# Head norms of a hybrid decoder layer gathered into one late block, and a weight load and a weight split moved

## The chip, the cores and the metric

The kernel runs on one core of one Trainium2 chip. The metric is the device time of one execution in microseconds (us); lower is better. Each kernel is timed in several runs, and the median is given. One further execution is profiled, which gives the rows below.

Of the core's engines, TensorE (PE in the profile) multiplies matrices into PSUM, VectorE (DVE), ScalarE (ACT) and GpSimd (POOL) do the rest, and SyncE (SP) issues the DMAs. Each engine takes its instructions in order, so one that waits holds all that are queued behind it. PEclk is the granted clock of TensorE as a share of the full one: 1.00 is 2.4 GHz, 0.50 is 1.2 GHz.

## The reference, cut to what matters

A decoder layer for 512 tokens of width 1024: a recurrent mixer (RG-LRU) and a sparse attention (NSA) in parallel, gates, then an MLP. All the projections come from one product with `w_in`. The part at hand is the root-mean-square norm over heads of 64 columns for the queries `q`, the selection keys `k_s` and the window keys `k_w`:

```python
def rmsnorm(x, g):
    xf = x.astype(jnp.float32)
    y = xf * lax.rsqrt(jnp.mean(xf * xf, axis=-1, keepdims=True) + NORM_EPS)
    return y.astype(x.dtype) * g

def nsa_mixer(q, k_c, v_c, k_s, v_s, k_w, v_w, ...):
    qh = rmsnorm(q.reshape(B, T, N_HEADS, hd), q_norm) * (hd ** -0.5)
    kc = rmsnorm(compress_blocks(kv(k_c), phi_k_pe, phi_k_w1, phi_k_w2), kc_norm)
    vc = compress_blocks(kv(v_c), phi_v_pe, phi_v_w1, phi_v_w2)
    ks = rmsnorm(kv(k_s), ks_norm)...
    kw = jnp.pad(rmsnorm(kv(k_w), kw_norm)...)

def hybrid_layer(x, ...):
    (u_rnn, u_gate, q, k_c, v_c, k_s, v_s, k_w, v_w, g_nsa, g_a, g_b) = jnp.split(xn @ w_in, cuts, axis=-1)
```

`compress_blocks` is a small two-layer network (weights `phi_*_w1`, `phi_*_w2`) over overlapping blocks of 32 tokens of `k_c` and `v_c`; its output is attended to as well.

## The kernel before, in words

Each product is made of three matmuls: a float32 operand is split into a rounded high part and the low rest, and high x high, high x low and low x high are summed in PSUM (`mm3`). So every weight tile, once loaded by a DMA into a raw buffer (`wraw`, two of them, filled by `raw`), is split by `split`: GpSimd or ScalarE copies out the high part (`wh`), then VectorE subtracts (`wl`). Two pairs of split buffers are in turn (WB = 2), so a split waits until TensorE has finished the tile two before.

The work runs in this order. First the 21 column tiles of the recurrent branch (`u_tiles`, in the order UO, loaded in pairs by `UW.load`), each followed by a causal convolution on VectorE (`uc`) whose rows are moved by DMAs into `ub`, and between them four blocks of the recurrence (`lru`), whose gate weights (`graw`) are loaded and split too. Then the token-major projections, by `tok_cols`: selection keys KS, selection values VS, window keys KW, window values and gates VW, and the first group of queries Q. Each uses all four PSUM banks named `lru`, one for each 128 tokens, and two or three weight pieces of at most 1024 columns. Its sink evicts the banks: `v_sink` copies the high part of the values by ScalarE and the low part by VectorE (both into `VV`); `head_norm` copies keys or queries by ScalarE (into `kn` or `qn`), squares them by ScalarE into a spare tile (`zdk` or `zdv`), and, after the last of the four banks, sums the squares by VectorE and normalizes. The norm itself is `rstd_heads`: the sum (VectorE), a scaling (VectorE), and a power of -0.5 (GpSimd, from the constant `halfs`); then VectorE multiplies each of the four blocks of 128x256.

Then come four column tiles for the compressed keys and values (class `Cols`, ZW, in the PSUM banks `mm`, with the high part copied by ScalarE), whose banks ScalarE and VectorE evict into `zdk` and `zdv`. After them comes compression itself: eight pieces of `phi_*_w1` loaded into `praw` (two buffers) and split into `pwh` and `pwl`, with matmuls of another product filled in between. Attention, the merge and the MLP follow and are as before.

The program is written in this order, but a scheduler places the instructions on each engine's queue by priorities; `tc.issue_after` holds an instruction back behind another. The queues are thus not those of the text, and the change is shown as they come out.

Of the kernel before, what the change touches and what calls it, by code (L numbers as in the profile page):

```python
# [11 lines left out]
F32 = mybir.dt.float32  # L12
F32R = mybir.dt.float32r
AF = mybir.ActivationFunctionType
# [54 lines left out]
def layer(ctx, tc, x, norm_mix, w_in, conv_w, conv_b, gate_a_w, gate_a_b, gate_x_w, gate_x_b,  # L69
# [58 lines left out]
    def split(v, a, b, pl=wp, tags=("wh", "wl"), prio=PRIO, bufs=WB, act=False):  # L128
        parts = v.shape[0]
        th = pl.tile([128, WH], F32R, name=tags[0], bufs=bufs)  # L130
        tl = pl.tile([128, WH], F32R, name=tags[1], bufs=bufs)
        h = th[:parts, :a * b].rearrange("p (a b) -> p a b", b=b)
        l = tl[:parts, :a * b].rearrange("p (a b) -> p a b", b=b)
        with tc.high_priority(offset=prio):
            if act:
                S.activation(h, v, AF.Copy)  # L136
            else:
                G.tensor_scalar(h, v, 1.0, 0.0, op0=OP.mult, op1=OP.add)  # L138
            split_last[0] = V.tensor_tensor(l, v, f32(h), op=OP.subtract).ins  # L139
        return h, l  # L140
# [101 lines left out]
    def u_half(n, hf):  # L242
        wh, wl = UW.get(n)
        run(feat_gen(p2[n], wh, wl, XH, XL, None, slice(256 * hf, 256 * hf + 256)))
# [6 lines left out]
    u_half(1, 0)  # L251
    u_half(0, 1)
    UW.load(2)
    u_half(1, 1)

    def col(src, name, parts, n):
# [256 lines left out]
    def rstd_heads(sq, nh, name, pl):  # L513
        ss = pl.tile([128, nh], F32, name=name, bufs=2)
        V.tensor_reduce(ss, sq, axis=AX, op=OP.add)
        V.tensor_scalar(ss, ss, 1.0 / 64, EPS, op0=OP.mult, op1=OP.add)
        G.tensor_tensor(ss, ss, halfs[:, :nh], op=OP.pow)
        return ss
# [39 lines left out]
        V.tensor_tensor(d4, d4, rs.unsqueeze(2).to_broadcast([128, 4, 64]), op=OP.mult)  # L558


    def head_norm(d, i, ps, pl, key):
        if i == 0:
            SQ[key] = pl.tile([128, 4, T], F32, name="zd" + "kvk"[key])[:, 0:2].rearrange("p a (b c) -> p (a b) c", c=256)
        src = ps[:, :256].rearrange("p (h d) -> p h d", d=64)
        S.activation(d[:, i], src, AF.Copy)
        S.activation(SQ[key][:, i], ps[:, :256], AF.Square)
        if i == 3:
            rs = rstd_heads(SQ.pop(key).rearrange("p i (h d) -> p (i h) d", d=64), 16, "hrs", pl)
            rv = rs.rearrange("p (i h) -> p i h", h=4)
            for n in range(4):  # L570
                V.tensor_tensor(d[:, n], d[:, n], rv[:, n].unsqueeze(2).to_broadcast([128, 4, 64]), op=OP.mult)

    def k_sink(br):
        def sink(i, ps):
# [79 lines left out]
    with pool("ph") as ph:  # L654
# [23 lines left out]
        for h in range(BC):  # L678
            bias_copies(h)
        tok_cols(COL_Q, 256, q_sink)  # L680
        w1p = {parts[0]: split(w1s.pop(parts[0]), 4, 256, ph, ("pwh", "pwl"), prio=0)}
        for n, nm in enumerate("kv"):
            z = ph.tile([128, 4, T], F32, name="zd" + nm)
            G.memset(z[64:128, :, 496:512], 0.0)
            for m in range(2):
                ps = psr.tile([128, T], F32, name="mm", bufs=3)
                wh, wl = ZW.get(2 * n + m)
                ZW.prep(2 * n + m + 1)
                run(feat_gen(ps, wh, wl, XH, XL, None))
                for gl in range(2):  # L690
                    g = 2 * m + gl
                    S.activation(z[0:64, g, :], ps[64 * gl:64 * gl + 64, :], AF.Copy)
                    V.tensor_copy(z[64:128, g, 0:496], ps[64 * gl:64 * gl + 64, 16:512])
            zd[nm] = z
        for nm, v in zip("kv", w2r):
            wh, wl = w2s[nm]
            S.activation(wh, v, AF.Copy)
            V.tensor_tensor(wl, v, f32(wh), op=OP.subtract)
# [591 lines left out]
```

## Time and profile before

| | us |
|---|---|
| median of 3 runs | 1060.33 (1060.20 to 1062.89) |
| the profiled execution | 1059.58 |
| its span in the trace | 1057.9 |
| TensorE busy | 1033.8 (98%) |
| VectorE busy | 647.4 (61%) |
| ScalarE busy | 388.6 (37%) |
| GpSimd busy | 310.3 (29%) |

The busy times are shares of the span. TensorE's is 98%, so the time is close to that of its matmuls, and the few stretches in which it rests or has a lower clock are to be looked for one by one. The stretch tables give each engine's busy time between two points; the rows of one engine in order of time tell what ended each wait.

### The profile page before, as it was taken

Reading aid. Unit: us, or ns where it says so; the run is one execution under the profiler, and the core shown is the slowest. Engines: PE = TensorE matmul, PEld = TensorE weight load, DVE = VectorE, ACT = ScalarE, POOL = GpSimd, SP = SyncE. Lnnn points to the kernel's source line nnn. Section 1 sums busy time; section 2 is a strip of 40 time slices with the busy share of each in tenths; the row PEclk is TensorE's granted clock in tenths of the full one; section 3 lists DMA queues with packets and bytes.
Section 4 is the critical chain, followed back from the end, with each engine's and each line's share of the span. In section 5 each row is a group of like instructions: output and inputs, shape, how many; then the busy total and the mean of one; then the engine's idle time right before and its main releaser. Section 6 shows DMA issues by size and latency. Waiting matters only on the chain.

```text
span 1057.9 us, 14717 instructions
## 1 busy us (share of the span) xinstructions
PE 1033.8 (98%) x5405; PEld 882.6 (83%) x5405; DVE 647.4 (61%) x1208; ACT 388.6 (37%) x808; POOL 310.3 (29%) x349
## 2 busy tenths in 40 slices
PE   6999999989999999999999999999999999999998
PEld 5777877989888898989988888888888888888886
DVE  5588989854764878868777669554333343444443
ACT  4356666413432666747657631132111111111010
POOL 4110111432231474546635423202111121111110
PEclk9999999989999999999999999999999999999999
DMA  7636333643263724334342278602323323323222
GB/s 181 147 94 197 87 108 117 140 126 126 66 189 100 229 78 122 118 114 119 69 132 91 91 243 301 210 1 80 111 89 91 109 83 116 120 80 103 97 80 80
DMA packets 110039, 127.89 MB, mean 121 GB/s; under 512 B 23087, under 2 KB 87375, under 8 KB 109967
## 3 DMA queue, kind: packets, MB, share of 16 engines
q1 hardware_dynamic: 109967, 126.94, 39.9%
q8 instruction: 43, 0.70, 0.3%
q14 instruction: 29, 0.24, 0.1%
HBM read 109.45 MB, written 15.64 MB: 118 GB/s over the span
## 4 chain that ended last, share of the span: by engine, by line
PE 90%; DVE 3%; DMA 2%; ACT 2%; issue 2%; POOL 1%; SPq 0%; DVEq 0%; ACTq 0%; POOLq 0%
PE mf L143 6%; PE mf L144 6%; PE mf L145 6%; PE am L145 5%; PE am L144 5%; PE am L143 5%; PE mi L145 5%; PE mi L143 5%; PE mi L144 5%; PE sc L922 4%; PE po L960 4%; PE pt L941 3%; PE mm L144 3%; PE mm L145 3%; PE mm L143 3%; PE lru L143 3%
## 5 line engine op out<-in xcount | busy, mean ns | idle before, releaser
L139 DVE TENSOR_TENSOR wl<-wraw,wh 128x1024 fp32r<-128x1024 f32 (+2 forms) x110 | 131.9, 1201 | 72.4 <-POOL wh L138 44.7
L138 POOL TENSOR_SCALAR wh<-wraw 128x1024 fp32r<-128x1024 f32 (+3 forms) x83 | 85.7, 1033 | 250.4 <-PE mi L144 119.1
L933 POOL TENSOR_SCALAR pp<-pp,sm,gates 128x512 f32<-128x512 f32 (+3 forms) x128 | 93.4, 737 | 68.0 <-DVE sm L931 45.2
L145 PE MATMUL am<-mwh,zl 128*128 128x512 f32 x256 | 99.3, 389 | 0.0
L144 PE MATMUL am<-mwl,zh 128*128 128x512 f32 x256 | 99.3, 389 | 0.0
L143 PE MATMUL am<-mwh,zh 128*128 128x512 f32 x256 | 98.8, 389 | 0.0
L145 PE MATMUL mi<-XH,wl 128*128 128x512 f32 x240 | 93.5, 390 | 0.3 <-DVE wl L139 0.3
L143 PE MATMUL mi<-XH,wh 128*128 128x512 f32 x240 | 93.5, 389 | 0.1
L144 PE MATMUL mi<-XL,wh 128*128 128x512 f32 x240 | 93.4, 389 | 0.0
L1233 DVE TENSOR_TENSOR zl<-Z,zh 128x512 fp32r<-128x512 f32 x32 | 36.2, 1134 | 88.4 <-ACT zh L1232 88.4
L143 PE MATMUL mm<-XH,wh 128*128 128x512 f32 (+1 forms) x216 | 81.9, 381 | 1.8 <-ACT wh L136 1.8
L144 PE MATMUL mm<-XL,wh 128*128 128x512 f32 (+1 forms) x216 | 81.7, 379 | 1.0 <-DVE XL L226 1.0
L930 ACT ACTIVATE pp<-pp,mx 128x512 f32<-128x512 f32 (+3 forms) x128 | 71.5, 561 | 29.3 <-DVE mx L928 27.2
L145 PE MATMUL mm<-XH,wl 128*128 128x512 f32 (+1 forms) x216 | 81.4, 378 | 0.5 <-DVE wl L139 0.5
L1206 DVE SCALAR_TENSOR_TENSOR Z<-mi,zr 128x512 f32<-128x512 f32 x30 | 20.7, 691 | 97.1 <-ACT zr L1205 97.1
L138 POOL TENSOR_SCALAR mwh<-wraw 128x1024 fp32r<-128x1024 f32 x32 | 34.0, 1062 | 138.4 <-PE am L145 131.3
L1232 ACT ACTIVATE zh<-Z 128x512 fp32r<-128x512 f32 x32 | 20.2, 632 | 136.5 <-PE am L144 134.4
L1205 ACT ACTIVATE zr<-mi 128x512 f32<-128x512 f32 x30 | 18.0, 600 | 141.7 <-PE mi L145 136.9
L928 DVE CUSTOM_DVE_ANT_0 pp<-sc,BT 128x512 f32<-128x512 f32 (+3 forms) x128 | 59.0, 484 | 15.3 <-PE pt L941 7.4
L947 ACT ACTIVATE PH<-pt 128x512 fp32r<-128x512 f32 (+1 forms) x96 | 49.3, 524 | 33.6 <-PE pt L941 33.1
L948 DVE TENSOR_TENSOR PL<-pt,PH 128x512 fp32r<-128x512 f32 (+1 forms) x96 | 55.9, 592 | 6.6 <-ACT PH L947 6.4
L922 PE MATMUL sc<-KK,QS 128*128 128x512 f32 (+3 forms) x256 | 57.8, 334 | 0.0
(299 smaller groups left out, 2687.1 us busy)
## 6 DMA issues: line engine op xcount, KB each, us to landing
wraw<-in_w_in_dram SPq DMA_DIRECT2D x26, 1024.0 KB, 5.2
wraw<-in_w_mlp_in_dram SPq DMA_DIRECT2D x16, 1024.0 KB, 5.6
wraw<-in_w_mlp_out_dram SPq DMA_DIRECT2D x16, 1024.0 KB, 4.8
tab_p<-tab_t SPq DMA_DIRECT2D x16, 320.0 KB, 5.0
wraw<-in_proj_a_dram SPq DMA_DIRECT2D x8, 640.0 KB, 5.3
BT<-tab_p SPq DMA_DIRECT2D x16, 256.0 KB, 2.8
wraw<-in_proj_b_dram SPq DMA_DIRECT2D x4, 1024.0 KB, 6.4
wraw<-in_w_out_dram SPq DMA_DIRECT2D x4, 1024.0 KB, 5.3
```

Of the source, the lines that this page charges most:

```text
L138: G.tensor_scalar(h, v, 1.0, 0.0, op0=OP.mult, op1=OP.add)
L139: split_last[0] = V.tensor_tensor(l, v, f32(h), op=OP.subtract).ins
L143: PE.matmul(ps, lh, rh, start=start, stop=False)
L144: PE.matmul(ps, lh, rl, start=False, stop=False)
L145: return PE.matmul(ps, ll, rh, start=False, stop=stop)
L922: ins = PE.matmul(ps[:, cs], grp.Q[r][:, ts], grp.K[br][:, hl, :128 * (i + 1)], start=hl == 0, stop=hl == 1)
L928: V.tensor_tensor_reduce(out=pp[:, cs], in0=ps[:, cs], in1=BTS[h][:, 384 - 128 * i:], scale=1.0, scalar=3e38, op0=OP.add, op1=OP.min, accu ...
L930: S.activation(pp[:, cs], pp[:, cs], AF.Exp, bias=mx, scale=-1.0, accum_out=sm)
L933: G.tensor_scalar(pp[:, cs], pp[:, cs], sm, gt, op0=OP.mult, op1=OP.mult)
L947: S.activation(ph, pv, AF.Copy)
L948: V.tensor_tensor(pl, pv, f32(ph), op=OP.subtract)
L960: PE.matmul(po[:, 128 * kt:], VV[:, kt, br, g], P[n][:, KT0[kt]:KT0[kt] + 128 * (4 - kt)], start=False, stop=br == 1 and kt == 3 and n == 1)
```

## The change

`head_norm` keeps the copy, the squares and the sum of squares, which it now writes into 16 of the 48 columns of one tile. A new function `head_norms` does the rest for KS, KW and Q together, and stands in the text behind the four column tiles of compression: scaling, a root by ScalarE (`AF.Sqrt`, which needs another activation table), a reciprocal, and one Newton step of four VectorE instructions, then the twelve multiplies. The power on GpSimd goes away for these three. The split of compression's first weight piece is to be issued behind the last split before it, that of the queries' second half. In the recurrent branch, the third pair of column weights is loaded earlier.

```diff
     u_half(0, 1)
     UW.load(2)
+    UW.load(4)
     u_half(1, 1)
...
+    SS, SD = [], []
+
     def head_norm(d, i, ps, pl, key):
...
         if i == 3:
-            rs = rstd_heads(SQ.pop(key).rearrange("p i (h d) -> p (i h) d", d=64), 16, "hrs", pl)
-            rv = rs.rearrange("p (i h) -> p i h", h=4)
+            if not SS:
+                SS.append(pl.tile([128, 48], F32, name="ss48"))
+            V.tensor_reduce(SS[0][:, 16 * key:16 * key + 16], SQ.pop(key).rearrange("p i (h d) -> p (i h) d", d=64),
+                            axis=AX, op=OP.add)
+            SD.append(d)
+
+    def head_norms(pl):
+
+        x, (r, t) = SS[0], (pl.tile([128, 48], F32, name=nm) for nm in ("rs48", "rt48"))
+        V.tensor_scalar(x, x, 1.0 / 64, EPS, op0=OP.mult, op1=OP.add)
+        S.activation(r, x, AF.Sqrt)
+        V.reciprocal(r, r)
+        V.tensor_tensor(t, r, r, op=OP.mult)
+        V.tensor_tensor(t, t, x, op=OP.mult)
+        V.tensor_scalar(t, t, -0.5, 1.5, op0=OP.mult, op1=OP.add)
+        V.tensor_tensor(r, r, t, op=OP.mult)
+        rv = r.rearrange("p (b i h) -> p b i h", b=3, h=4)
+        for b, d in enumerate(SD):
             for n in range(4):
-                V.tensor_tensor(d[:, n], d[:, n], rv[:, n].unsqueeze(2).to_broadcast([128, 4, 64]), op=OP.mult)
+                V.tensor_tensor(d[:, n], d[:, n], rv[:, b, n].unsqueeze(2).to_broadcast([128, 4, 64]), op=OP.mult)
...
         tok_cols(COL_Q, 256, q_sink)
-        w1p = {parts[0]: split(w1s.pop(parts[0]), 4, 256, ph, ("pwh", "pwl"), prio=0)}
+        with tc.issue_after(split_last[0]):
+            w1p = {parts[0]: split(w1s.pop(parts[0]), 4, 256, ph, ("pwh", "pwl"), prio=0)}
...
             zd[nm] = z
+        head_norms(ph)
```

VectorE's queue from the last weight split of VS (the first row) to the second of KW, before:

```order
L139 TENSOR_TENSOR wl<-wraw,wh 128x1024
L515 TENSOR_REDUCE hrs<-zdk 128x16
L516 TENSOR_SCALAR hrs<-hrs 128x16
L571 TENSOR_TENSOR kn<-kn,hrs 128x4x64 x4
L139 TENSOR_TENSOR wl<-wraw,wh 128x1024
L582 TENSOR_TENSOR VV<-lru,VV 128x4x64
L139 TENSOR_TENSOR pwl<-praw,pwh 128x1024
L582 TENSOR_TENSOR VV<-lru,VV 128x4x64
...
L139 TENSOR_TENSOR pwl<-praw,pwh 128x1024
L582 TENSOR_TENSOR VV<-lru,VV 128x4x64 x2
L139 TENSOR_TENSOR wl<-wraw,wh 128x1024
```

And now:

```order
L139 TENSOR_TENSOR wl<-wraw,wh 128x1024
L573 TENSOR_REDUCE ss_1798<-zdk 128x16
L139 TENSOR_TENSOR wl<-wraw,wh 128x1024
L601 TENSOR_TENSOR VV<-lru,VV 128x4x64 x2
...
L601 TENSOR_TENSOR VV<-lru,VV 128x4x64 x2
L139 TENSOR_TENSOR wl<-wraw,wh 128x1024
```

The scaling, the four multiplies and both splits of compression weights have left the stretch; left out are two short splits (`w2lk`, `w2lv`) that stand in both. GpSimd's queue loses the power there and is else the same.

VectorE's queue from the splits for the first two column tiles of compression (the first row) on, before:

```order
L139 TENSOR_TENSOR wl<-wraw,wh 128x1024 x2
L515 TENSOR_REDUCE hrs<-zdk 128x16
L516 TENSOR_SCALAR hrs<-hrs 128x16
L139 TENSOR_TENSOR wl<-wraw,wh 128x1024
L693 COPY zdk<-mm 64x496
L571 TENSOR_TENSOR qn<-qn,hrs 128x256 x4
L693 COPY zdk<-mm 64x496
L139 TENSOR_TENSOR wl<-wraw,wh 128x1024
```

And now, from the scaling on:

```order
L580 TENSOR_SCALAR ss_1798<-ss_1798 128x48
L582 RECIPROCAL rs_2452<-rs_2452 128x48
...
L586 TENSOR_TENSOR rs_2452<-rs_2452,rt_2453 128x48
L590 TENSOR_TENSOR kn<-kn,rs_2452 128x4x64 x6
L139 TENSOR_TENSOR wl<-wraw,wh 128x1024
L590 TENSOR_TENSOR kn<-kn,rs_2452 128x4x64 x2
L590 TENSOR_TENSOR qn<-qn,rs_2452 128x256 x3
L713 COPY zdk<-mm 64x496
L590 TENSOR_TENSOR qn<-qn,rs_2452 128x256
L139 TENSOR_TENSOR wl<-wraw,wh 128x1024
```

The new block with its twelve multiplies stands ahead of and between the splits for the third and the fourth column tile. ScalarE's queue has the table load and the root just ahead of its copy (`wh`) for the third column tile, and a table load between the square and the tanh of compression's first activation.

SP's queue of DMAs among the constants and the gate weights, before:

```order
L276 DMA kcg<-in_kc_norm_dram 64x1 x2
...
L287 DMA pev<-in_phi_v_pe_dram 64x16x1 x2
L121 DMA graw<-in_gate_a_w_dram 112x3x336
L121 DMA graw<-in_gate_x_w_dram 112x3x336
L121 DMA wraw<-in_w_in_dram 128x8x256 x2
L341 DMA ub<-uc 112x512
```

And now:

```order
L277 DMA kcg<-in_kc_norm_dram 64x1
L121 DMA wraw<-in_w_in_dram 128x8x256
L277 DMA kcg<-in_kc_norm_dram 64x1
...
L121 DMA graw<-in_gate_a_w_dram 112x3x336
L121 DMA graw<-in_gate_x_w_dram 112x3x336
L121 DMA wraw<-in_w_in_dram 128x8x256
L342 DMA ub<-uc 112x512
```

One of the two loads of 1 MB behind the gate weights now stands between the two loads of `kcg`.

## Rows read from the trace of the kernel before

**Rows 1.** Stretch table: stretch, length, busy PE, PEld, DVE, ACT, POOL, clock, DMA.

```profile
41.40:44.90 3.50, 1.24 (x4) 0.77 (x5) 1.79 (x2) 2.67 (x3) 0.00 (x0) 1.00 1.10 333
44.90:206.90 162.00, 161.93 (x770) 131.09 (x769) 139.53 (x203) 96.21 (x135) 27.25 (x29) 1.00 0.41 118
...
213.40:218.35 4.95, 0.14 (x2) 0.03 (x1) 4.95 (x6) 0.38 (x1) 3.07 (x3) 0.92 0.02 3
218.35:224.45 6.10, 6.10 (x28) 6.10 (x29) 4.66 (x8) 0.00 (x0) 0.00 (x0) 0.50 0.62 140
224.45:300.00 75.55, 75.55 (x470) 68.81 (x469) 43.32 (x67) 26.46 (x58) 20.83 (x19) 1.00 0.42 124
```

**Rows 2.** TensorE in order of time: start, duration, instruction, idle before and releaser.

```profile
207.64 0.39 PE L144 MATMUL lru<-wl,XH 128*128 128x256 f32 x1 [0.58 <-DVE wl L139]
...
213.14 0.28 PE L144 MATMUL lru<-wl,XH 128*128 128x256 f32 x1
213.26 0.28 PE L145 MATMUL lru<-wh,XL 128*128 128x256 f32 x1
218.35 0.55 PE L143 MATMUL lru<-wh,XH 128*128 128x256 f32 x1 [4.82 <-DVE VV L582]
...
268.63 0.39 PE L143 MATMUL mm<-XH,wh 128*128 128x512 f32 x1
...
274.07 0.39 PE L143 MATMUL mm<-XH,wh 128*128 128x512 f32 x1
```

**Rows 3.** VectorE in order of time, at the start of KW.

```profile
211.96 4.78 DVE L571 TENSOR_TENSOR kn<-kn,hrs 128x256 f32<-128x256 f32 x4 [3.03 <-POOL hrs L517]
216.66 1.21 DVE L139 TENSOR_TENSOR wl<-wraw,wh 128x1024 fp32r<-128x1024 f32 x1
```

**Rows 4.** GpSimd in order of time, in the same stretch.

```profile
209.01 2.92 POOL L517 TENSOR_TENSOR hrs<-hrs,halfs 128x16 f32<-128x16 f32 x1 [2.20 <-DVE hrs L516]
...
212.91 2.39 POOL L138 TENSOR_SCALAR pwh<-praw 128x1024 fp32r<-128x1024 f32 x2
```

**Rows 5.** Early stretch, each in time: SP, POOL, ACT, DVE; page's and 0:62's loads.

```profile
24.96 1.77 SPq L276 DMA_DIRECT2D kcg<-in_kc_norm_dram  x2
...
33.71 1.05 SPq L121 DMA_DIRECT2D wraw<-in_w_in_dram  x2
...
39.10 1.03 POOL L138 TENSOR_SCALAR gwh<-graw 112x1008 fp32r<-112x1008 f32 x1 [0.62 <-DMA graw<-in_gate_x_w_dram]
46.38 0.62 POOL L368 TENSOR_SCALAR uh<-ub 112x512 fp32r<-112x512 f32 x1 [6.24 <-DMA ub<-uc]
...
42.02 1.06 ACT L136 ACTIVATE wh<-wraw 128x1024 fp32r<-128x1024 f32 x1 [9.94 <-DMA wraw<-in_w_in_dram]
...
48.84 0.74 DVE L335 SCALAR_TENSOR_TENSOR uc<-mm,cw,uc 128x509 f32<-128x509 f32 x1
...
wraw<-in_w_in_dram SPq DMA_DIRECT2D x26, 1024.0 KB, 5.2
...
wraw<-in_w_in_dram SPq DMA_DIRECT2D x4, 1024.0 KB, 7.2
```

**Rows 6.** VectorE in order of time, behind the queries.

```profile
261.40 0.17 DVE L516 TENSOR_SCALAR hrs<-hrs 128x16 f32<-128x16 f32 x1
...
265.51 0.67 DVE L693 COPY zdk<-mm 64x496 f32<-64x496 f32 x1
266.21 1.43 DVE L571 TENSOR_TENSOR qn<-qn,hrs 128x256 f32<-128x256 f32 x4
```

**Rows 7.** ScalarE in order of time: a table load, and compression's first activation.

```profile
156.12 1.28 ACT L391 ACT_TABLE_LOAD   x1
157.41 1.49 ACT L391 ACTIVATE rr<-rr 112x1536 f32<-112x1536 f32 x1
...
297.88 0.36 ACT L323 ACTIVATE hs<-lru 128x256 f32<-128x256 f32 x1
300.06 0.42 ACT L325 ACTIVATE hs<-hs 128x256 f32<-128x256 f32 x1 [1.82 <-DVE hs L324]
```

## The prediction, made from the trace of the kernel before

> **What bounds the kernel now.** I read the stretch table first, since shares of the whole span hide where TensorE rests. From 44.9 to 206.9 us TensorE is busy for 161.93 of 162.00 us, and from 224.45 to 300 for all of it [rows 1]. So what the matmuls need is the bound, and the change can win only where TensorE waits or runs slowly. Two such places lie where the diff works. In the stretch 41.4 to 44.9 TensorE is busy for 1.24 of 3.50 us. From 213.4 to 218.35 it is busy for 0.14 of 4.95, and from 218.35 to 224.45 it is busy throughout, but at a granted clock of 0.50: 28 matmuls in 6.10 us [rows 1]. Next I read TensorE's own rows at these places, for the releaser. The matmuls for the window keys (columns KW) start at 218.35, after 4.82 us, released by VectorE's eviction of VV; the last matmul before them is at 213.26 [rows 2]. Then VectorE and GpSimd in the same stretch: GpSimd takes 2.92 us from 209.01 for one power of 128x16, and VectorE, which waits 3.03 us for it, then needs 4.78 us for the four multiplies of kn [rows 3, 4]. Only behind them come KW's weight split, at 216.66, and the evictions of VV [rows 3]. TensorE needs both, as one of the four PSUM banks must be free and its weights must be there. So a short norm, in the middle of an in-order queue, holds TensorE.
>
> **The pause before KW.** The change leaves only the sum of squares there and puts power, wait and multiplies behind the first queries. From VectorE's queue go the small scaling, 3.03 us of waiting and 4.78 of multiplies, nearly 8 us [rows 3]. I follow what is late next, in the clock of the trace before. KW's first weight half needs a buffer that the first half of VS gives back just ahead of the matmul at 207.64 [rows 2]. GpSimd, no longer in a power, copies it at once, in about 1.2 us as its other copies [rows 4]; VectorE's sum of squares ends by 208.8 (211.96 - 3.03 - 0.17, the wait and the scaling [rows 3, 6]), its split of 1.21 us by 210.0, and the first VV follows. TensorE asks for them at 213.26 + 0.12 = 213.38, matmuls coming every 0.12 us there [rows 2], so 3 us are to spare. KW's second half gets its buffer at 213.4, is ready 2.4 us later (copy and split), and is wanted 48 matmuls on, at 219.1. Compression's first two copies stay where they are in GpSimd's queue (2.39 us from 212.91 before [rows 4], now about 3 us earlier) and end before that. Only their VectorE halves, 2.4 us, move behind the queries' second weight half. The loads that follow them in SP's queue move too: four loads of compression weights go behind three loads of column weights; they serve the work after the last column tile, which ends at 274.07 + 5.44 [rows 2]. The pause of 218.35 - 213.38 = 4.97 us is gone. So, if TensorE does not rest, is the slow clock: 28 matmuls at full clock are 28 x 0.12 = 3.36 us, against 6.10, so 2.74 more [rows 1]. A shorter pause earlier in this trace, 41.4 to 44.9, left the clock at 1.00 [rows 1]. **7.7 us** in sum; the lower bound is nothing (third rival), the upper is 7.7 + 0.58, the wait at 207.64 that VectorE's backlog causes [rows 2].
>
> **The early load.** The third pair of weight columns is now issued after the first kcg load, at about 25.6, and not at 33.7 [rows 5]. Before, ScalarE waited 9.94 us for it, to 42.02 [rows 5], and TensorE rested for 3.50 - 1.24 = 2.26 [rows 1]. Now ScalarE's copy is set by a buffer that TensorE frees one tile earlier (5.44 us, from 268.63 to 274.07 [rows 2]), at about 36, so that pause goes. What it costs: the load takes an issue slot (0.5 us) ahead of the small constants, and the eighth DMA after it, a pev load, waits for its landing. Eleven issues filled the time from 25.6 to 33.7, 0.74 each, so that one comes at about 31.5. By the page's median of 5.2 us the pair lands at 30.8 and holds nothing; by 7.2, the median of the kernel's start, at 32.8, and what follows is issued 1.3 us later [rows 5]. For it, one megabyte less stands between the gate weights, landed at 39.10, and the ub copies: up to 42.02, so 2.9 us. GpSimd's first use of ub, at 46.38, moves 2.9 - 0.5 = 2.4 us earlier, or 1.1 in the bad case. This matters because VectorE's uc at 48.84, queued behind it, frees the PSUM bank for the next tile but one [rows 5]. TensorE's own rest of 2.26 and VectorE's 2.4 meet: **2.3 us**, between 1.1 and 2.9; I take the upper half, since only small constants move when the load is issued.
> Whether it lasts: TensorE is full to 206.9, but VectorE is busy for 139.5 of these 162 us [rows 1], and its late split makes the wait of 0.58 at 207.64 [rows 2]. All of VectorE's work there follows from work that has moved by about the same 2.3, so I keep it.
>
> **The norms' new place.** Behind the queries VectorE now does: sum of squares (as before), scaling to 261.57 [rows 6], then, after ScalarE's root, a reciprocal and four steps on 128x48, six multiplies of kn, the split for the third column tile of compression, two more kn, three qn, a copy, one qn, the next split. No row shows a root or a reciprocal of that size. The nearest, the scaling of 128x16, took 0.17 us, and a multiply of 128x256 goes every 1.43 / 4 = 0.36 [rows 6]. Six steps are 1.0 to 2.2 us; with hand-overs I take 1.2, near the smaller, as 48 columns are nearer to 16 than to 256. The 0.36 is with GpSimd quiet; a multiply of kn under GpSimd's copies took 4.78 / 4 = 1.20 [rows 3, 4]. I take 0.36: GpSimd's power goes away, and its next copy waits for the buffer that TensorE gives back at 274.07. So 261.57 + 1.2 + 6 x 0.36 + 1.21 = 266.1, needed at 268.63 [rows 2]: 2.5 us of cover, 1.5 with the dearer steps. The next split: six multiplies, a copy of 0.67 and 1.21 more [rows 6], 270.2, needed at 274.07. Cost nothing. ScalarE's copy for the third tile, now behind the root, had to wait for its buffer to 268.63 - 5.44 = 263.2 anyway.
> Two table loads come in. In this trace a load takes 1.28 us, and the activation after it starts 0.01 us later, at 157.41 [rows 7]. The first runs beside VectorE's sum of squares. The second stands between the square at 297.88 and the tanh at 300.06, where ScalarE sat for 1.82 us [rows 7]. Cost nothing.
> The Trainium skill, page "ScalarE: Activation LUTs", section "What ACT_TABLE_LOAD costs", speaks against it: besides 1283 ns it counts a drain of about 1380 ns, 2.66 us for each change of tables. The trace agrees with the first number and shows no drain. By the page's sum the tanh would start near 300.9 and not 300.06, an estimate from that page, and the forecast would be later by under 1 us.
>
> **The sum.** The profiled execution took 1059.58 us. 1059.6 - 7.7 - 2.3 = 1049.6. The median of the runs shown is 1060.33, 0.75 above; on that scale **1050.3**. Behind the column tiles nothing is added or moved but a table load, so no step of the change can give the gain back later.
>
> **Rivals.**
> First, the early gain is lost by 207: VectorE's backlog does not move with TensorE, and the wait at 207.64 grows from 0.58 to 2.9. For it: VectorE's share of that stretch [rows 1]. Against: TensorE had no other wait in 162 us. Price 2.3: 1052.6.
> Second, the norms become the wait. The fourth tile's split is ready at 261.57 + 1.2 + 12 m + 2 x 1.21 + 2 x 0.67 (with the second copy, which frees its bank) = 266.5 + 12 m, m being one multiply, and is needed at 274.07 [rows 2, 6]; from m = 0.63 TensorE waits. At the 1.20 of [rows 3] the loss is 6.9: 1057.2. It ends slower than before from m = 1.46, where 12 m - 7.5 eats 10.0; at one GpSimd copy of 1.20 [rows 4] in front of each multiply, m = 1.62, the loss is 11.9: 1062.2. For it: the kn rows under GpSimd's copies. Against: GpSimd has nothing to copy there.
> The Trainium skill, page "SBUF — State Buffer", section "Who interferes with whom", names the mechanism: a VectorE instruction with two SBUF inputs and a GpSimd instruction that reads SBUF block each other for a whole instruction. The trace agrees, 1.20 against 0.36; the rule needs GpSimd to be reading, and no run here shows that for the new place.
> Third, the change does not do what it says before KW: something else on GpSimd or SP (the compression weights' landing ahead of KW's second copy) holds TensorE as long, and the clock falls again. Only the early 2.3 is left: 1058.0. Against: 3 us to spare on either half.
>
> **How the numbers follow.** Forecast 0.63; first rival 0.20; second at 1057.2, 0.05, and at 1062.2, 0.05; third 0.07. The forecast's own range goes by gains of 7.7 + 1.1 to 7.7 + 2.9 + 0.58: 1049.1 to 1051.5. With the first rival, and 1.4 us more for a short wait of the norms, it is 1048.6 to 1054.0; the second and third rival, 0.17, stay out. About 0.3% (3.2 us, to 1057.1) is what a measurement of this kernel can tell from no change: faster 0.89, the same 0.08 (third rival and most of the second), slower 0.03.
>
> **What would show it.** TensorE without a pause between VS and KW, and a clock of 1.00 there; KW's weight split on VectorE within 3 us of the sum of squares. No pause near 41, and the tile after next about 2 us earlier. A wait at the VS second half of 0.6, not 2.9. Twelve multiplies of some 0.4 us behind the queries, with no wait of TensorE at the third or fourth column tile. The prediction is wrong if TensorE waits there, if the clock is 0.50 anywhere in 205 to 225, or if a pause stands before KW with another releaser.

## The result, and the profile after

| | before | after |
|---|---|---|
| median, us | 1060.26 (1058.26 to 1062.89, 4 runs) | 1050.75 (1049.61 to 1052.73, 4 runs) |
| the profiled execution | 1059.58 | 1050.31 |
| its span | 1057.9 | 1048.6 |

After to before is 0.9915, 95% interval 0.9895 to 0.9934: 9.0 us less by this ratio. A second measurement, below, gave 0.9916 (0.9896 to 0.9936).

The stretch table of the changed kernel, to be laid beside [rows 1] (busy us of each engine with instructions in brackets, TensorE's granted clock, share of the DMA engines, GB/s):

```profile
core 0: us, PE busy (x) PEld busy (x) DVE busy (x) ACT busy (x) POOL busy (x), PEclk, DMA share, GB/s
41.20:44.90 3.70, 3.70 (x18) 3.08 (x17) 0.05 (x1) 1.04 (x2) 0.71 (x2) 1.00 0.81 227
44.90:204.60 159.70, 158.59 (x756) 128.28 (x754) 139.51 (x201) 95.55 (x135) 26.18 (x28) 1.00 0.43 118
204.60:211.00 6.40, 5.81 (x48) 5.70 (x48) 4.63 (x8) 1.58 (x5) 3.94 (x3) 1.00 1.12 253
211.00:216.00 5.00, 5.00 (x44) 5.00 (x43) 1.91 (x3) 0.38 (x1) 1.05 (x1) 1.00 0.31 93
216.00:225.00 9.00, 9.00 (x74) 9.00 (x74) 2.66 (x3) 2.64 (x8) 2.07 (x3) 1.00 0.41 107
225.00:290.00 65.00, 65.00 (x385) 58.34 (x384) 44.58 (x75) 26.71 (x54) 12.86 (x14) 1.00 0.50 137
```

From 211 to 290 TensorE is busy throughout and the clock is 1.00: the pause before KW and the slow clock behind it are gone. So is the rest near 41, where ScalarE had waited 9.94 us for its weights [rows 5]. In the 159.7 us from 44.9, 1.11 us of rest are new. TensorE's rows say where that is (the wait for `uc`, called tile 5 below), and that the wait at the second half of VS has its old size (0.58 in [rows 2]):

```profile
47.38 0.47 PE L143 MATMUL mm<-XH,wh 128*128 128x512 f32 x1 [1.11 <-DVE uc L336]
...
205.31 0.38 PE L144 MATMUL lru<-wl,XH 128*128 128x256 f32 x1 [0.59 <-DVE wl L139]
```

VectorE around KW, against [rows 3]: the sum of squares, KW's first weight split 1.13 us later, the first VV behind it, and, after the row of dots, KW's second split. GpSimd's power is not there to be waited for.

```profile
205.18 1.20 DVE L573 TENSOR_REDUCE ss<-zdk 128x16 f32<-128x1024 f32 x1
206.31 1.21 DVE L139 TENSOR_TENSOR wl<-wraw,wh 128x1024 fp32r<-128x1024 f32 x1
207.44 0.41 DVE L601 TENSOR_TENSOR VV<-lru,VV 128x256 fp32r<-128x256 f32 x1
...
212.37 1.23 DVE L139 TENSOR_TENSOR wl<-wraw,wh 128x1024 fp32r<-128x1024 f32 x1 [0.29 <-POOL wh L138]
```

VectorE and ScalarE at the norms' new place, against [rows 6] (the first block is VectorE, the second ScalarE):

```profile
251.24 0.19 DVE L580 TENSOR_SCALAR ss<-ss 128x48 f32<-128x48 f32 x1
251.74 0.45 DVE L582 RECIPROCAL rs<-rs 128x48 f32<-128x48 f32 x1 [0.31 <-ACT rs L581]
...
252.94 0.21 DVE L586 TENSOR_TENSOR rs<-rs,rt 128x48 f32<-128x48 f32 x1
253.18 2.11 DVE L590 TENSOR_TENSOR kn<-kn,rs 128x256 f32<-128x256 f32 x6
255.20 1.22 DVE L139 TENSOR_TENSOR wl<-wraw,wh 128x1024 fp32r<-128x1024 f32 x1
...
259.53 1.23 DVE L139 TENSOR_TENSOR wl<-wraw,wh 128x1024 fp32r<-128x1024 f32 x1 [0.28 <-ACT wh L136]
```

```profile
249.38 1.28 ACT L581 ACT_TABLE_LOAD   x1
251.46 0.24 ACT L581 ACTIVATE rs<-ss 128x48 f32<-128x48 f32 x1 [0.80 <-DVE ss L580]
...
288.00 1.28 ACT L326 ACT_TABLE_LOAD   x1
289.81 0.42 ACT L326 ACTIVATE hs<-hs 128x256 f32<-128x256 f32 x1 [0.52 <-DVE hs L325]
```

The six multiplies of kn take 0.35 us each. The splits for the third and fourth column tiles are done at 256.42 and 260.76. TensorE wants them at 258.43 and 263.87 (268.63 and 274.07 of [rows 2], less the 10.2 us by which this stage has moved) and does not wait. The second table load, at 288.00, ends at 289.28, and the tanh waits for VectorE after that; before, ScalarE sat there as long without it [rows 7].

### The profile page after: what moved, and what is told of

It is laid out like the page before. It is cut to its first block, busy times and chain, and to the rows that moved or that the text cites. A ratio compares the mean times of both kernels' runs of the same rounds, so it can differ in the third digit from the quotient of the medians.

```text
span 1048.6 us, 14720 instructions
## 1 busy us (share of the span) xinstructions
PE 1030.1 (98%) x5405; PEld 879.2 (84%) x5405; DVE 646.4 (62%) x1211; ACT 391.2 (37%) x811; POOL 299.9 (29%) x346
## 4 chain that ended last, share of the span: by engine, by line
PE 84%; DMA 5%; DVE 5%; issue 2%; ACT 2%; POOL 1%; SPq 0%; DVEq 0%; POOLq 0%; ACTq 0%
PE mf L143 6%; PE mf L144 6%; PE mf L145 6%; PE am L145 6%; PE am L143 6%; PE am L144 6%; PE mi L145 5%; PE mi L143 5%; PE mi L144 5%; PE sc L943 4%; PE po L981 4%; PE pt L962 3%; PE mm L144 3%; PE mm L143 3%; PE mm L145 3%; PE lru L143 3%
```

## Three stages, fourteen traces

To compare executions I cut the program at four of TensorE's waits that every trace has: the second half of VS, the transposes of `hg` near 300, the wait for `spl` near 330, and the first `mi` wait near 715. Stage A runs from the span's start to the first, B lies between the first two, C between the last two. What lies between B and C is 30.7 us in every trace, and what follows C is 340.9 before and after. Each number is the start of a matmul (A) or the difference of two such starts (B, C). "Rests" are TensorE's waits of 0.2 us and more after 41 us, without those that all have (0.6 to 1.3 at VS, 0.8 at `hg`, 0.56 at `spl`, and some 0.8 in sum from 698 on).

| kernel (runs below) | A | B | C | rests, us |
|---|---|---|---|---|
| before | 207.64 | 93.91 | 384.71 | 1.78 and 0.53 near 44; 4.82 before KW |
| after | 205.31 | 85.99 | 385.72 | 1.11 at tile 5; 0.32 at 671 |
| early | 207.31 | 92.74 | 386.05 | 1.96 at tile 5; 4.82 before KW; 0.58 at 680 |
| norms | 207.24 | 86.01 | 385.17 | 2.10 and 0.53 near 43 |
| split | 207.67 | 93.90 | 386.33 | 1.07 and 0.53 near 43; 4.84 before KW; 0.66 at 611; 0.42 at 682 |
| late_power | 205.21 | 86.58 | 386.48 | 1.18 at tile 5; 0.6 more at `hg`; 0.44 at 601; 0.74 at 672 |
| old_root | 208.99 | 89.52 | 384.99 | 2.47 and 0.53 near 43; 0.88, 0.23 before and in KW; 1.26 at 243 |
| hold4 | 205.43 | 91.62 | 386.17 | 1.08 at tile 5; 2.68 before KW; 0.44 at 349; 0.41 at 677 |
| hold6 | 205.45 | 92.24 | 386.83 | 4.60 before KW; 1.69 at 678 |
| gp_copies | 207.49 | 90.64 | 387.24 | 2.15 at tile 5; 2.75 at 269; 1.69 at 679 |
| again | 207.83 | 86.00 | 385.48 | 2.00 at tile 5 |
| late_pe | 204.50 | 86.00 | 384.95 | none |
| out_split | 205.69 | 85.95 | 385.89 | 1.26 at tile 5; 0.43 at 601 |
| both | 204.71 | 86.00 | 385.96 | 0.44 at 342; 0.27 at 600 |

For the two profiled executions the account is 2.33 won in A, 7.92 in B, 1.01 given back in C: 9.24 of the 9.27 between 1059.58 and 1050.31. Of the 1.01 in C, 0.48 are waits of TensorE (0.32 near 671, 0.15 near 601); for the rest the same 2267 matmuls are busy 0.5 us longer, and no row says why.

## Experiments: the parts one by one

**early**: the kernel before with the early load alone.

```diff
     UW.load(2)
+    UW.load(4)
     u_half(1, 1)
```

> The kernel before with the early load of the third weight pair and nothing else. By the forecast's parts (each pays by itself): the rest of TensorE near 41 us goes, tile 5 starts 2.35 us earlier (47.38 instead of 49.73), and the gain is still there at 205 us, so the pause before KW stays 5 us long, its slow clock stays, and the time is 1058.0, 2.3 below before. Rival (the backlog of VectorE at the end of the first stretch eats it, or the pause before KW, which VectorE and GpSimd set, does not move with TensorE): 1060.3.

Measured: 1058.86 against 1060.59 (ratio 0.9984, 0.9973 to 0.9995), 1.7 less, with an interval of 0.5 to 2.9. The pause before KW is as it was, 4.82 us. In the profiled execution A is only 0.3 shorter, for the rest near 43 has become a longer one at tile 5:

```profile
49.13 0.47 PE L143 MATMUL mm<-XH,wh 128*128 128x512 f32 x1 [1.96 <-DVE uc L336]
```

So the load pays by itself. The mean is less than the forecast's 2.3, which the interval does not exclude.

**norms**: the changed kernel without that load.

```diff
     UW.load(2)
-    UW.load(4)
     u_half(1, 1)
```

> The changed kernel without the early load: the norms late in one piece, and the split moved. By the forecast's parts: no pause before KW and a clock of 1.00 there, 7.7 us below before, 1052.6; the wait at the second half of VS stays at 0.58. Rival (the two parts need each other, since only together they keep VectorE ahead): less than 7 or more than 9 us. The 1.0 us that the changed kernel gave back behind 590 us: if it belongs to the norms' part, it is lost here too and the time is 1053.6 or so; if it depends on the exact shift of the later stages, another amount is lost.

Measured: 1054.10, ratio 0.9933 (0.9917 to 0.9950), 7.1 less than before by the ratio; B is 86.01. The two parts add up: 0.9984 x 0.9933 = 0.9917, against 0.9915 and 0.9916 for both together. The profiled execution, the fastest of the four, lost 0.46 in stage C and not 1.0.

**split**: the kernel before with compression's first splits moved, the norms left.

```diff
-        w1p = {parts[0]: split(w1s.pop(parts[0]), 4, 256, ph, ("pwh", "pwl"), prio=0)}
+        with tc.issue_after(split_last[0]):
+            w1p = {parts[0]: split(w1s.pop(parts[0]), 4, 256, ph, ("pwh", "pwl"), prio=0)}
```

> The kernel before with compression's first two splits issued behind the queries' second weight half, as in the changed kernel, and nothing else; the norms stay where they were. By the forecast the power, its wait and the multiplies make the pause before KW, and the two splits (2.4 us of VectorE) stand behind KW's weight split: the pause stays near 5 us at a clock that falls to 0.50, and the time is that of before, 1060.3, within 1. Rival (the splits, or their loads and GpSimd's copies, hold VV's evictions or KW's second half): the pause shrinks by up to 2.4 us, 1057.9 or, if the clock holds, 1055.2.

Measured: 1061.53, ratio 1.0005 (0.9994 to 1.0016). TensorE waits as before, for the same releaser:

```profile
218.39 0.55 PE L143 MATMUL lru<-wh,XH 128*128 128x256 f32 x1 [4.84 <-DVE VV L582]
```

B is 93.90 against 93.91. The moved splits alone bring nothing. No run has the norms late and the splits left in place, so whether the late norms need the move stays open.

**late_power**: the changed kernel with the power on GpSimd at the late place.

```diff
-        S.activation(r, x, AF.Sqrt)
-        V.reciprocal(r, r)
-        V.tensor_tensor(t, r, r, op=OP.mult)
...
+        V.memset(t, -0.5)
+        G.tensor_tensor(r, x, t, op=OP.pow)
```

> The changed kernel with its late place for the norms, but with GpSimd's power on 48 columns in place of the root, the reciprocal and the Newton step. The planner then puts the third and fourth splits of the column tiles ahead of the multiplies. Theory 1, the place alone brings the gain: no pause before KW, and the power, at 2.9 us for 16 columns some 8 to 9 us long, holds only GpSimd, which has copies to do for buffers that come free later: 1050.8. Theory 2, the root is needed too, because a power of this length holds GpSimd's copies of the next weights or the multiplies: TensorE waits between 260 and 300 us for weights or copies, up to 5 us, 1052 to 1056.

Measured: 1051.27, ratio 0.9910 (0.9896 to 0.9925), the same as the changed kernel. The power of 48 columns takes 8.04 us, and GpSimd's next copy waits for TensorE anyway. VectorE's splits now stand ahead of the multiplies (GpSimd first, then VectorE):

```profile
251.51 8.04 POOL L582 TENSOR_TENSOR rs<-ss,rt 128x48 f32<-128x48 f32 x1
```

```profile
254.00 1.23 DVE L139 TENSOR_TENSOR wl<-wraw,wh 128x1024 fp32r<-128x1024 f32 x1 [2.66 <-ACT wh L136]
...
259.44 1.23 DVE L139 TENSOR_TENSOR wl<-wraw,wh 128x1024 fp32r<-128x1024 f32 x1 [2.17 <-ACT wh L136]
...
261.39 2.77 DVE L586 TENSOR_TENSOR kn<-kn,rs 128x256 f32<-128x256 f32 x8
```

At this place the method costs 0.6 us of B (0.57 more wait for `hg`) and no time that the runs can tell. The place is what pays. The split at 254.00 runs inside the power, from 251.51 to 259.55, and takes its usual 1.23 us: this GpSimd instruction, which reads two tiles in SBUF, does not slow VectorE.

**old_root**: the kernel before, norms at their old places, by root and Newton step.

```diff
-            rs = rstd_heads(SQ.pop(key).rearrange("p i (h d) -> p (i h) d", d=64), 16, "hrs", pl)
+            x, rs, t = (pl.tile([128, 16], F32, name=nm, bufs=2) for nm in ("hrs", "rs16", "rt16"))
+            V.tensor_reduce(x, SQ.pop(key).rearrange("p i (h d) -> p (i h) d", d=64), axis=AX, op=OP.add)
+            V.tensor_scalar(x, x, 1.0 / 64, EPS, op0=OP.mult, op1=OP.add)
+            S.activation(rs, x, AF.Sqrt)
+            V.reciprocal(rs, rs)
...
+            V.tensor_tensor(rs, rs, t, op=OP.mult)
```

> The kernel before with its norms where they were, but each by ScalarE's root, a reciprocal and a Newton step on 16 columns in place of GpSimd's power. The 3.03 us for which VectorE waits go down to about 0.3 and five short steps of some 0.2; the four multiplies stay ahead of KW's weight split, at 0.36 each if GpSimd is quiet and at up to 1.26 if its copies run beside them. So the pause before KW shrinks from 4.82 to between 0 and 3.3 us. Theory 1, the place decides: a rest of the pause stays (the nearer to 3 the more of the multiplies run beside GpSimd's copies), and the time is 1054 to 1059. Theory 2, the power was the whole cause: no pause, and the time is that of the changed kernel without its early load, 1052.6 to 1054.

Measured: 1056.82, ratio 0.9960 (0.9945 to 0.9974), 4.6 less: half of the gain. The pause before KW shrinks to 0.88, as the first theory said. Outside what I had expected, a new wait comes at 243: the tanh of the gates follows a root here, and its table load stands between evictions that TensorE waits for (ScalarE, then TensorE at both waits):

```profile
241.45 1.28 ACT L592 ACT_TABLE_LOAD   x1
242.74 0.31 ACT L592 ACTIVATE gates<-lru 128x48 f32<-128x48 f32 x2
```

```profile
215.77 0.35 PE L143 MATMUL lru<-wh,XH 128*128 128x256 f32 x1 [0.88 <-DVE VV L590]
...
243.09 0.36 PE L143 MATMUL lru<-wh,XH 128*128 128x256 f32 x1 [1.26 <-ACT gates L592]
```

So a table load is free only where nobody waits for what stands behind it. The Trainium skill, page "ScalarE: Activation LUTs", section "What ACT_TABLE_LOAD costs", gives a drain of about 1380 ns beside the load's 1283. The trace agrees with the load and not with the drain: from 241.45 to 242.74 are 1.29 us.

## Experiments: how the pause becomes a slow clock

**hold4** and **hold6** are the changed kernel with the sum of squares of the first keys repeated, four and six times, and the evictions of VV and KW's split kept behind it. No power, no wait for GpSimd and no multiplies are there. This is hold4's edit without the lines that keep the order; hold6 has 7 in place of the 5:

```diff
-            V.tensor_reduce(SS[0][:, 16 * key:16 * key + 16], SQ.pop(key).rearrange("p i (h d) -> p (i h) d", d=64),
-                            axis=AX, op=OP.add)
+            sq = SQ.pop(key).rearrange("p i (h d) -> p (i h) d", d=64)
+            for _ in range(5 if key == 0 else 1):
+                red = V.tensor_reduce(SS[0][:, 16 * key:16 * key + 16], sq, axis=AX, op=OP.add)
```

> The changed kernel with the sum of squares of the first keys done five times instead of once, 4 x 1.20 us more on VectorE ahead of KW's weight split and of VV's evictions. The changed kernel has its first VV evicted at 207.85 and wants it at 211.05, so 3.2 us are to spare and the pause is 4.8 - 3.2 = 1.6 us. If such a pause leaves TensorE's granted clock at 1.00, it costs itself: 1052.4. Rival (any pause here brings the slow clock, 1.3 to 3.4 us as the traces of before and of the early load alone had it): 1053.7 to 1055.8.

Measured: 1053.69 (1052.98 to 1056.51), ratio 0.9933 (0.9915 to 0.9950). The pause is 2.68 and not 1.6: the five sums took 6.22 us, and the split behind them 2.08 instead of 1.21, with one of GpSimd's copies beside it. TensorE's first row after the pause and the clock of the profiled execution:

```profile
214.00 0.55 PE L143 MATMUL lru<-wh,XH 128*128 128x256 f32 x1 [2.68 <-DVE VV L610]
```

```profile
214.00:217.00 3.00, 3.00 (x14) 3.00 (x15) 2.38 (x6) 0.00 (x0) 0.00 (x0) 0.50 0.00 0
217.00:222.00 5.00, 5.00 (x32) 5.00 (x32) 0.00 (x0) 0.00 (x0) 0.00 (x0) 0.68 0.86 224
```

The clock is at 0.50, the lower of its two levels, for some 6 us. But this execution is the longest of the four; its mean clock is 0.997, while two others have 1.000 over the whole span at 1052.98 and 1053.55. So at this place the slow clock comes in some executions and not in others; how long the pause was in those two is not known, as they were not profiled.

> The changed kernel with the sum of squares of the first keys done seven times, 6 x 1.20 us more on VectorE, and two small splits of 0.9 us that now stand ahead of the last one: 8.1 - 3.2 = 4.9 us of pause before KW, as in the kernel before, but with no power, no GpSimd wait and no multiplies there. If the pause alone makes the slow clock, the granted clock falls to 0.50 behind it, and the whole costs 4.9 + 1.3 to 3.4: 1057.0 to 1059.1. Rival (the slow clock has another cause, such as the evictions or GpSimd's power): 1055.7.

Measured: 1057.43, ratio 0.9965 (0.9952 to 0.9978). The time is in the range of the first theory but does not decide, since the kernel before took 1061.46 beside it, 1.2 more than in the result. The clock decides. The pause is 4.60 us, the clock falls behind it, and the mean clock lies between 0.994 and 0.998 in all five executions:

```profile
215.93 0.55 PE L143 MATMUL lru<-wh,XH 128*128 128x256 f32 x1 [4.60 <-DVE VV L610]
```

```profile
215.90:219.00 3.10, 3.07 (x14) 3.10 (x15) 2.01 (x4) 0.00 (x0) 0.00 (x0) 0.50 0.02 2
219.00:222.00 3.00, 3.00 (x27) 3.00 (x26) 0.00 (x0) 0.00 (x0) 0.00 (x0) 0.97 0.93 233
```

So a pause of this length is enough, without the power and the multiplies. What it costs beyond itself is B less 86.0 less the pause: 3.1 before (93.91 - 86.00 - 4.82), 3.1 in split, 1.9 in early, 2.9 in hold4, 1.6 in hold6. The mean clock of all 41 executions of the kernel before that were timed beside these experiments lies between 0.994 and 0.998. On a span of 1058 us, 0.001 of it is 2.1 us at half speed, 1.06 us lost if TensorE is busy: at most 2 to 6 us in each, by this estimate. The profiled one's 0.996 would be 4.2, where stage B shows 3.1.

## Experiment: copies on GpSimd beside the multiplies

**gp_copies** gives GpSimd something to do where the second rival needed it.

```diff
         V.tensor_tensor(r, r, t, op=OP.mult)
+        gt = pl.tile([128, T], F32, name="gtst")
+        G.tensor_scalar(gt[:, :48], r, 1.0, 0.0, op0=OP.mult, op1=OP.add)
+        for k in range(16):
+            G.tensor_scalar(gt, f32(XH[:, k % 8]), 1.0, 0.0, op0=OP.mult, op1=OP.add)
```

> The changed kernel with 16 copies of 128x512 on GpSimd, from SBUF to SBUF, that start when the norms' roots are done, so that fourteen of them run beside the twelve multiplies; VectorE's order is the same. Theory (second rival of the prediction): the multiplies lengthen from 0.36 to between 0.9 and 1.2 us. VectorE's split for the third column tile comes 6 x 0.54 to 6 x 0.84 later, 3.2 to 5.0, against 2.0 to spare in the changed kernel, and the fourth's 12 x 0.54 to 12 x 0.84 later, 6.5 to 10, against 3.1: TensorE waits 3.4 to 7 us in sum, 1054 to 1058. Rival: GpSimd's copies do not reach VectorE there, the multiplies stay at 0.36 and the time at 1050.8.

Measured: 1056.19 (1054.85 to 1058.68), ratio 0.9947 (0.9930 to 0.9964), against 0.9915 for the changed kernel: 3.4 us by the ratios (5.4 by the medians, but the kernel before was 1.2 slower here). VectorE, GpSimd and TensorE:

```profile
255.38 3.79 DVE L594 TENSOR_TENSOR kn<-kn,rs 128x256 f32<-128x256 f32 x6
259.08 1.63 DVE L139 TENSOR_TENSOR wl<-wraw,wh 128x1024 fp32r<-128x1024 f32 x1
...
262.13 2.33 DVE L594 TENSOR_TENSOR qn<-qn,rs 128x256 f32<-128x256 f32 x3
...
265.83 1.63 DVE L139 TENSOR_TENSOR wl<-wraw,wh 128x1024 fp32r<-128x1024 f32 x1
267.49 2.00 DVE L717 COPY zdk<-mm 64x496 f32<-64x496 f32 x3
```

```profile
255.97 11.96 POOL L590 TENSOR_SCALAR gtst<-XH 128x512 f32<-128x512 f32 x14
...
268.70 1.31 POOL L590 TENSOR_SCALAR gtst<-XH 128x512 f32<-128x512 f32 x2
```

```profile
269.01 0.47 PE L143 MATMUL mm<-XH,wh 128*128 128x512 f32 x1 [2.75 <-DVE zdk L717]
```

```profile
269.00:274.00 5.00, 4.99 (x15) 3.97 (x16) 3.70 (x7) 2.93 (x6) 0.93 (x2) 0.66 0.37 125
```

The multiplies lengthen from 0.35 to 0.63 and 0.78, a split from 1.22 to 1.63, and GpSimd's copies from 0.66 (the last two, beside VectorE's copies from PSUM) to 0.85. The mechanism is there, smaller than the 0.9 to 1.2 that I took from the kn rows, where GpSimd's copies were twice as large (128x1024); that size was not tried here. TensorE waits 2.75 us, not at the third tile but for the copy of `zdk` behind the fourth split, which frees its bank. B is 4.64 longer; the other 1.9 is the slow clock, 0.66 from 269 to 274. This execution is the longest of the four, and two others have a mean clock of 1.000.

The Trainium skill, page "SBUF — State Buffer", section "Who interferes with whom", says that the two engines lock a shared port against each other. The traces agree that both get slower. The 0.28 to 0.43 us that a multiply loses here are less than one whole copy. Six multiplies (2.11 us when quiet) and some 4.4 copies (0.66 each) pass in 3.79 us, where one after the other they would take 5.0; and the split inside the power of late_power lost nothing. So a lock for a whole instruction, as the prediction has it, is not what these rows show.

## Experiments: the start, the late stage, and a better version

**again** is the changed kernel once more, nothing altered.

> The changed kernel once more, nothing altered: how much of a stage differs from one execution to the next. Theory 1, the 1.0 us given back behind 590 us and the start's gain belong to the kernel: TensorE's wait for the last split of the output weights is about 0.3 again, tile 5 starts near 47.4, the time is 1050.8. Theory 2, both hang on when single transfers land, as the spread over the traces so far says (that wait 0 to 1.7 us, tile 5's start 47.3 or 49.1 with the early load): they come out elsewhere in these ranges, and the time is 1050 to 1052.5.

Measured: 1052.60 (1049.70 to 1053.39, 6 runs), ratio 0.9916 (0.9896 to 0.9936): theory 2, though 0.1 above its range. The wait for the last output split is absent, and C is 385.48. But tile 5 waits 2.00 us instead of 1.11, and this time the clock falls behind it:

```profile
48.30 0.47 PE L143 MATMUL mm<-XH,wh 128*128 128x512 f32 x1 [2.00 <-DVE uc L336]
```

```profile
45.00:52.00 7.00, 5.00 (x17) 3.64 (x16) 5.89 (x7) 2.32 (x3) 2.90 (x3) 0.80 0.25 58
```

With the early load A has two groups: 205.2 to 205.7 in after, late_power, hold4, hold6 and out_split, 207.3 to 207.8 in early, gp_copies and again. Without it: 207.2 to 207.7, and 209.0 in old_root, where the clock fell behind a rest of 2.47. In gp_copies GpSimd's copy of the gate weights starts at 39.92, in after at 38.51, and the ub copies behind them land 1.6 us later. In hold6 there is no rest at tile 5, yet A is as in after: what stands before it ran later (ScalarE's copy of the weights of the early load starts at 36.45, in after at 35.20). So A is not that rest alone. Mean with the load 206.2 (eight traces, the two with altered loads left out), without 207.9: 1.7, as the times of early say.

**late_pe**: the changed kernel with compression's position columns loaded behind the copies of uc to ub, the last of which `UBL` holds.

```diff
-            SP.dma_start(t[64 * j:64 * j + 64], src[0, 16 * j:16 * j + 16].rearrange("l d -> d l"))
...
     u_tiles(5, 6)
+    with tc.issue_after(UBL[0]):
+        for nm, src in (("k", phi_k_pe), ("v", phi_v_pe)):
+            for j in range(2):
+                SP.dma_start(pe2[nm][64 * j:64 * j + 64], src[0, 16 * j:16 * j + 16].rearrange("l d -> d l"))
```

> The changed kernel with the four loads of compression's position columns (pek and pev, 0.7 us of issuing each) behind the first copies of uc to ub, instead of ahead of the gate weights. The gate weights and the fourth weight pair are issued 3 us earlier, the ub copies behind them land about 2 us earlier, and TensorE's wait for uc at tile 5 (1.1 us, or 2.1 where the transfers land late) goes: 1.1 to 2.1 less, 1048.7 to 1049.7. Rival (the copies wait for uc itself or for bytes, not for the queue): 1050.8.

Measured: 1048.84 (1047.74 to 1050.03, 6 runs), ratio 0.9889 (0.9872 to 0.9907). The gate weights are issued at 29.92 instead of 33.58 and GpSimd has ub at 40.31 instead of 44.19 (SP, then GpSimd):

```profile
29.92 0.58 SPq L121 DMA_DIRECT2D graw<-in_gate_a_w_dram  x1
```

```profile
40.31 1.82 POOL L367 TENSOR_SCALAR uh<-ub 112x512 fp32r<-112x512 f32 x2 [2.72 <-DMA ub<-uc]
```

```profile
45.00:52.00 7.00, 7.00 (x33) 5.72 (x32) 6.30 (x9) 2.18 (x3) 1.97 (x3) 1.00 0.22 57
52.00:204.00 152.00, 151.92 (x727) 123.04 (x725) 128.84 (x189) 93.33 (x131) 24.36 (x25) 1.00 0.46 122
```

TensorE does not rest from 41 to 204 but for 0.08 us; with the rest the slow clock at the start is gone: the mean clock is 0.999 or 1.000 in all 11 executions of late_pe and both, but 0.998 in four of the ten of the changed kernel. By the medians this version is 3.8 us below the changed kernel on the same chip, and 1.9 below its first measurement; the single times are 1047.74 to 1050.03 against 1049.61 to 1053.39 in both measurements, so the two hardly overlap.

**out_split**: the last copy and split of the output weights (`ow_last`) ahead of the MLP's first two.

```diff
         for m in range(2):
-            wh, wl = MW.get(m)
+            with tc.issue_after(ow_last[0]), tc.issue_after(ow_last[1]):
+                wh, wl = MW.get(m)
```

> The changed kernel with the copies and splits of the first two weight tiles of the MLP put behind the last copy and split of the output weights on GpSimd and VectorE, instead of ahead of them. If TensorE's wait near 670 us comes from the landing of the MLP's first load, in front of which GpSimd stands with the last copy of the output weights behind it, the wait goes in every run: 0.6 less by the mean of the traces so far, 1050.2, and the stage from the wait at 322 to the wait at 707 takes 384.7 to 385.2. Rival (the wait has another cause): it stays between 0 and 1.7.

**both**: this and late_pe.

> The changed kernel with both of these: position columns loaded later, and the last split of the output weights ahead of the MLP's. If the two pay by themselves: 1.7 to 2.7 less than the changed kernel, 1048.1 to 1049.1. Rival (what is won at the start is eaten later, by the backlog at 205 us): 1050.

In the changed kernel GpSimd's last copy for the output weights stands behind two copies that wait for the MLP's load; TensorE waits for its split:

```profile
664.44 2.07 POOL L138 TENSOR_SCALAR wh<-wraw 128x1024 fp32r<-128x1024 f32 x2 [5.68 <-DMA wraw<-in_w_mlp_in_dram]
666.48 2.02 POOL L138 TENSOR_SCALAR owh<-wraw 128x1024 fp32r<-128x1024 f32 x1
```

```profile
670.76 0.50 PE L144 MATMUL ao<-owl,MH 128*128 128x512 f32 x1 [0.32 <-DVE owl L139]
```

In hold6 the load was issued and landed later within the stage: counted from the start of C, GpSimd's first copy starts at 343.47 (671.89 in the trace) against 342.42 in after, and TensorE's wait is 1.69. In again it starts at 342.16, and the wait is absent. In out_split the last output copy starts at 663.90 and the MLP's at 665.22, and neither out_split nor both shows the wait. But C is 385.89 and 385.96, not below 385.2: smaller waits near 342 and 600 come up instead. The times are 1050.86 (0.9911, 0.9893 to 0.9929) and 1048.87 (0.9888, 0.9871 to 0.9906), the latter as late_pe alone. Where the wait comes from is shown by the rows; that its removal pays is not.

## Why the prediction was right, step by step

The forecast was 1050.3, within 1048.6 to 1054.0; measured were 1050.75 and 1052.60. By the ratios the gain is 9.0 and 8.9 us, where 10.0 were forecast. That the first median came within 0.5 us is in part chance.

- **The pause before KW**, 4.97 (4.82 by the releaser's row): gone. The first VV was out at 207.85 and wanted at 211.03, the second half split at 213.60 and wanted 48 x 0.12 later, at 216.8. The 3 us to spare on either were 3.2. The third rival did not happen. split and late_power show that the norms' place did this, not the moved split alone and not the root, which at the old place left 0.88 (old_root).
- **The slow clock**, 2.74: right in kind, as hold6 shows. In the profiled pair it was 3.1; over six traces with a pause there or at 269 it was 1.6 to 3.1. The sentence that a shorter pause at 41 "left the clock at 1.00" was true of that execution, and of norms (2.10) and gp_copies (2.15 at tile 5), but not of again (2.00) or old_root (2.47): one trace with a rest of this length does not settle the clock.
- **The early load**, 2.3: 2.33 in the profiled pair, by the route described: ScalarE's copy at 35.20 (36 said), GpSimd's use of ub 2.19 earlier (2.4 said), uc next late. On the mean it is 1.7, by the traces and by early's times. So the term looks mis-sized, in the choice of "the upper half": when the gate weights land differs by 1.4 us from one trace to another, and the ub copies stand behind them. The first rival did not happen, the wait at VS stayed at 0.6.
- **The norms' new place**, 0: right. The term for the small steps was too small: from the end of the scaling at 251.43 to the first multiply at 253.18 are 1.75 us, not 1.2, since the reciprocal of 48 columns takes 0.45 and VectorE waits 0.31 for the root. The cover was 2.0 and 3.1 instead of 2.5 and 3.9. gp_copies shows that the second rival's condition, GpSimd copying beside the multiplies, does cost time, at 0.63 to 0.78 a multiply and not 1.20 with copies of 128x512.
- **Two table loads**, 0: right at these two places, and old_root shows a place where it isn't.
- **"No step of the change can give the gain back later"**: the profiled pair gave back 1.01 in C. Fourteen traces have C between 384.71 and 387.24, and the kernel before has the lowest, 1.2 under the mean of the others (385.94). The part near 671 hangs on when one load lands. A chance low of C would account for the 0.75 us by which the profiled execution of before lay under the median, and which the forecast put back in; one trace of before can't show it. What the change itself does to C, if anything, is smaller than this spread and stays open.
- **Sums**: at one copy of 1.20 in front of each multiply of 0.36, m is 1.56 and not 1.62, and the second rival's dear end 1061.5 and not 1062.2. The lower end 1048.6 is 0.5 below the forecast's own 1049.1, and nothing says why. By the prices given, all of the second and third rival lie within the 3.2 us that a measurement can't tell, so "faster" would be 0.83 and "the same" 0.17.

## What to carry to other kernels

A short in-order step with a cross-engine wait should stand where its results are next needed, not where its inputs are ready: here the place paid 7.1 us with the root (norms) and about as much with the power (late_power, less the early load), and the cheaper method at the old place 4.6. A pause of TensorE is to be priced with the clock that may fall behind it, and a rest of 2 us that costs only itself in one trace may bring the slow clock in the next (gp_copies and again, at tile 5). Before an early stage is priced from one profile, ask which waits end with a transfer: those move by 1 to 2 us from one execution to the next.

## What the runs showed of the hardware that I had not expected

- In the profiled executions the granted clock stayed at 1.00 behind rests of TensorE of 1.96 (early), 2.10 (norms) and 2.15 us (gp_copies, tile 5), and fell to 0.50 behind 2.00 (again), 2.47 (old_root), 2.68 (hold4) and 2.75 (gp_copies, at 269). Behind 4.6 us and more it fell each time, and the mean clock was below 1.000 in every execution (hold6, before).
- GpSimd's power takes 2.92 us for 16 columns [rows 4] and 8.04 for 48; VectorE's reciprocal of 48 columns takes 0.45, of 16 columns 0.25 (old_root). A split of 128x1024 inside the power took 1.23 us, as without it (late_power).
- Four loads of 4 KB each take 3.4 us of SP's queue (30.19 to 33.58 in after). Without them ahead, the gate weights were issued 3.7 us earlier, and TensorE's wait at tile 5 went (late_pe).
